# Patch extraction (im2col) on one core: two larger loads, stores of two channels throughout, and copies of three planes in one instruction

## Chip, cores, metric

One core of a Trainium2 chip. The metric is the device time of one execution in microseconds (us). The profile's span, from the first to the last instruction, is shorter than the device time of the same run (90.1 against 91.84). Most runs of one kernel agree within a few tenths of a per cent; a run over 1.5% above the fastest of its kernel counts as slow and is left out of the ratios.

## The reference, cut to what matters

```python
x = randn(16, 64, 32, 32) float32;  kernel_size = 3
for b in range(16):
    for i in range(30):
        for j in range(30):
            cols[b, :, i * 30 + j] = x[b, :, i:i+3, j:j+3].ravel()      # cols: (16, 576, 900) float32
```

Nothing is computed. Each input channel (32 × 32) appears nine times in the output, as nine planes of 30 × 30: plane (ki, kj) is the window that starts at row ki and column kj. 4.19 MB are read and 33.18 MB are written.

## The kernel before

Each of the 128 partitions holds eight channels (32 KB). For each channel nine copies build the planes in an output tile, and the tile goes out in long contiguous runs. There are two output buffers of two channels each, and all transfers are issued from one queue (SP).

```python
in_tile = in_pool.tile([P, CPP, H, W], x.dtype, name="in_tile")          # CPP = 8 channels
out_pool = ctx.enter_context(tc.tile_pool(name="out_pool", bufs=2))
cuts = [0, H, 200, CPP * H]                     # 4 KB, 21 KB and 7 KB per partition
first = load(nc.sync, cuts[0], cuts[1])
bulk = load(nc.sync, cuts[1], cuts[2])
load(nc.sync, cuts[2], cuts[3])

on_act = (False, True, False, True, False)
n = 0
for c in range(0, CPP, 2):
    out_tile = out_pool.tile([P, 2, KK, HO, WO], x.dtype, name="out_tile")
    for s in range(2):
        for kk in range(KK):
            ki, kj = divmod(kk, K)
            src = in_tile[:, c + s, ki : ki + HO, kj : kj + WO]
            dst = out_tile[:, s, kk]
            if on_act[n % len(on_act)]:
                nc.scalar.copy(out=dst, in_=src)
            else:
                nc.vector.tensor_copy(out=dst, in_=src)
            n += 1
        if c == 0:
            st = nc.sync.dma_start(out=out_v[:, s], in_=out_tile[:, s]...)      # one channel
            if s == 0:
                tc.add_manual_dep(st.ins, bulk.ins.name, ...,
                                  reason="the store follows the bulk of the loads")
    if c > 0:
        nc.sync.dma_start(out=out_v[:, c : c + 2]..., in_=out_tile...)          # two channels
# ... afterwards the first load is moved to the head of the program
```

## Time and profile before

| | kernel before |
|---|---|
| device time, median of the 6 runs taken with the changed kernel | 91.72 us (91.44 to 92.87, the highest counted as slow; medians of later rounds 91.54 to 91.56) |
| span of the profiled run (device time 91.84 us) | 90.1 us |
| VectorE / ScalarE busy | 23.5 / 26.2 us |
| DMA engines busy | 97.0% |
| first load packet / first store packet / last packet's end | 1.01 / 11.54 / 88.78 us |

How to read it: the two copy engines idle most of the time, the DMA engines hardly ever. The times of the last line come from the packet records of the trace (each packet's size, start and duration). The profiled run is 0.3 us above the later medians. Its records show one reason: 33 of the 128 packets of the bulk load (21,504 bytes) took 0.83 to 1.38 us instead of 0.80, which adds up to 0.24 us on each DMA engine, at a time when no store had been issued. No run here shows why. The prediction shows the profile's own lines.

### The profile page before, as it was taken

The page shows a single profiled execution, that of the slowest core. Times are in us where ns is not written, and L with a number is a line of the kernel's source. Part 1 is how long each engine was busy: PE and PEld are TensorE (multiplying, and loading weights), DVE is VectorE, ACT ScalarE, POOL GpSimd, SP SyncE. Part 2 cuts the span into 40 slices and gives each one's busy share as a digit, 9 for nine tenths or more (in the row PEclk, how much of TensorE's full clock was granted, in tenths as well). Part 3 has the DMA queues.
Part 4 walks back from the last instruction along what each step waited for, and adds up shares of the span by engine and source line. Part 5 has one row for each costly group of instructions (what it writes and reads, how often), then busy time and mean ns, then how long its engine had stood idle before and what let it go on. Part 6 is the DMA issues. An engine that isn't in the chain of part 4 may idle for free.

```text
span 90.1 us, 140 instructions
## 1 busy us (share of the span) xinstructions
DVE 23.5 (26%) x43; ACT 26.2 (29%) x30; POOL 0.2 (0%) x4
## 2 busy tenths in 40 slices
DVE  0380399970000089600000399300000000000000
ACT  5391399940000089920000399300000000000000
POOL 0000000000000000000000000000000000000000
DMA  5999899999599999993799999999999999947990
GB/s 129 486 382 449 360 518 446 460 460 446 259 460 460 691 460 432 460 432 173 345 460 460 460 460 460 460 460 460 460 460 460 460 432 460 403 201 345 460 460 0
DMA packets 1152, 37.37 MB, mean 415 GB/s; under 512 B 128, under 2 KB 128, under 8 KB 384
## 3 DMA queue, kind: packets, MB, share of 16 engines
q1 hardware_dynamic: 1152, 37.37, 97.0%
HBM read 4.19 MB, written 33.18 MB: 415 GB/s over the span
## 4 chain that ended last, share of the span: by engine, by line
DMA 45%; DVE 16%; DVEq 1%; issue 0%; SPq 0%
DMA out_dram<-out_tile 35%; DVE out_tile L57 16%; DMA in_tile<-in_x_dram 11%; DVEq L93 1%; DVEq L57 0%; SPq L75 0%
## 5 line engine op out<-in xcount | busy, mean ns | idle before, releaser
L55 ACT COPY out_tile<-in_tile 128x900 f32<-128x900 f32 x29 | 24.9, 938 | 30.1 <-DMA out_dram<-out_tile 25.3
L57 DVE COPY out_tile<-in_tile 128x900 f32<-128x900 f32 x43 | 23.5, 624 | 33.6 <-DMA out_dram<-out_tile 26.0
L55 ACT ACT_TABLE_LOAD x1 | 1.3, 1283 | 0.8 <-PEq L122 0.8
L122 POOL MEMSET const-bfloat16-1.0<- 128x1 bf16 x1 | 0.1, 102 | 0.0
L122 POOL MEMSET const-uint8-127<- 128x1 uint8 x1 | 0.1, 102 | 0.0
L122 POOL MEMSET const-float32-0.0<- 128x1 f32 x1 | 0.1, 99 | 0.2 <-issue 0.2
L122 POOL MEMSET const-float32-1.0<- 128x1 f32 x1 | 0.1, 99 | 0.0
## 6 DMA issues: line engine op xcount, KB each, us to landing
out_dram<-out_tile SPq DMA_DIRECT2D x3, 8100.0 KB, 31.3
out_dram<-out_tile SPq DMA_DIRECT2D x2, 4050.0 KB, 14.9
in_tile<-in_x_dram SPq DMA_DIRECT2D x1, 2688.0 KB, 9.6
in_tile<-in_x_dram SPq DMA_DIRECT2D x1, 896.0 KB, 11.4
in_tile<-in_x_dram SPq DMA_DIRECT2D x1, 512.0 KB, 3.6
```

The source lines that it names most:

```text
L55: nc.scalar.copy(out=dst, in_=src)
L57: nc.vector.tensor_copy(out=dst, in_=src)
L93: tc.compile()
L122: nc = _bacc.Bacc("TRN2", target_bir_lowering=False, num_devices=1)
```

## The change

The intent: fewer and larger operations. Two loads instead of three (8 and 24 KB per partition, cut into packets of at most 12 KB), four equal stores of two channels each, and 28 copies of up to three planes instead of 72 of one. The three windows of one row offset ki start at columns 0, 1 and 2, so a source view with a leading step of one element covers all three; the three planes of the destination are neighbours.

```diff
-    cuts = [0, H, 200, CPP * H]
-    first = load(nc.sync, cuts[0], cuts[1])
-    bulk = load(nc.sync, cuts[1], cuts[2])
-    load(nc.sync, cuts[2], cuts[3])
+    first = load(0, 2 * H)                  # both with max_dma_last_dim=12288
+    load(2 * H, CPP * H)
+
+    def windows(c, ki, kj, n):
+        w = in_tile[:, c, ki : ki + HO, kj : kj + WO]
+        part, row, col = [list(d) for d in w.ap]
+        return bass.AP(w.tensor, w.offset, [part, [1, n], row, col])
 
-    on_act = (False, True, False, True, False)
-    n = 0
+    units = (                               # channel of the pair, ki, kj, planes, on ScalarE?
+        (0, 0, 0, 3, False),
+        (0, 1, 0, 3, True),
+        (0, 2, 0, 3, False),
+        (1, 0, 0, 3, True),
+        (1, 1, 0, 3, False),
+        (1, 2, 2, 1, True),
+        (1, 2, 0, 2, False),
+    )
     for c in range(0, CPP, 2):
         out_tile = out_pool.tile([P, 2, KK, HO, WO], x.dtype, name="out_tile")
-        ... nine single-plane copies per channel; at c == 0 one store per channel,
-            the first of them with a wait on the bulk load; at c > 0 one store per pair
+        for s, ki, kj, n, on_act in units:
+            src = windows(c + s, ki, kj, n)
+            dst = out_tile[:, s, ki * K + kj : ki * K + kj + n]
+            if on_act:
+                nc.scalar.copy(out=dst, in_=src)
+            else:
+                nc.vector.tensor_copy(out=dst, in_=src)
+        nc.sync.dma_start(out=out_v[:, c : c + 2]..., in_=out_tile...)
```

More of the change, by code (lines that the diff above doesn't have):

```diff
@@ L19, in _im2col @@
     CPP = B * C // P
-    assert CPP * P == B * C and C % CPP == 0 and CPP % 4 == 0
+    assert CPP * P == B * C and C % CPP == 0 and CPP % 2 == 0 and K == 3
     x_v = x.rearrange("b (cp c2) h w -> (b cp) (c2 h w)", c2=CPP)
@@ L31, in _im2col, with load @@
     in_flat = in_tile.rearrange("p c h w -> p (c h w)")
-    def load(queue, r0, r1):
-        return queue.dma_start(
-            out=in_flat[:, r0 * W : r1 * W], in_=x_v[:, r0 * W : r1 * W]
-        )
-    cuts = [0, H, 200, CPP * H]
-    first = load(nc.sync, cuts[0], cuts[1])
-    bulk = load(nc.sync, cuts[1], cuts[2])
-    load(nc.sync, cuts[2], cuts[3])
-    on_act = (False, True, False, True, False)
-    n = 0
+    def load(r0, r1):
+        return nc.sync.dma_start(
+            out=in_flat[:, r0 * W : r1 * W],
+            in_=x_v[:, r0 * W : r1 * W],
+            max_dma_last_dim=12288,
+        )
@@ L48, in _im2col @@
         out_tile = out_pool.tile([P, 2, KK, HO, WO], x.dtype, name="out_tile")
-        for s in range(2):
-            for kk in range(KK):
-                ki, kj = divmod(kk, K)
-                src = in_tile[:, c + s, ki : ki + HO, kj : kj + WO]
-                dst = out_tile[:, s, kk]
-                if on_act[n % len(on_act)]:
-                    nc.scalar.copy(out=dst, in_=src)
-                else:
-                    nc.vector.tensor_copy(out=dst, in_=src)
-                n += 1
-            if c == 0:
-                st = nc.sync.dma_start(
-                    out=out_v[:, s],
-                    in_=out_tile[:, s].rearrange("p kk i j -> p (kk i j)"),
-                )
-                if s == 0:
-                    tc.add_manual_dep(
-                        st.ins,
-                        bulk.ins.name,
-                        mybir.DependencyInfo(
-                            mybir.DependencyClass.Sync, mybir.DependencyReason.DATA
-                        ),
-                        reason="the store follows the bulk of the loads",
-                    )
@@ L74, in _im2col @@
-        if c > 0:
-            nc.sync.dma_start(
-                out=out_v[:, c : c + 2].rearrange("p c n -> p (c n)"),
-                in_=out_tile.rearrange("p c kk i j -> p (c kk i j)"),
-            )
+        for s, ki, kj, n, on_act in units:
[5 more added lines that the diff above has]
+                nc.vector.tensor_copy(out=dst, in_=src)
@@ L79, in _im2col @@
+        nc.sync.dma_start(
+            out=out_v[:, c : c + 2].rearrange("p c n -> p (c n)"),
+            in_=out_tile.rearrange("p c kk i j -> p (c kk i j)"),
+        )
     return first
```

## The prediction

The recorded text is cut where that is marked: what it said of the hardware without a trace of this case is gone, and with it terms of the forecast's sum. What they came to: 2.97 us for a copy of three planes on VectorE and 1.09 for one of two, which make the 9.7 us per pair, and 2.44 us for three planes on ScalarE, which make the 5.6. The whole sum then runs 4.8 + 9.7 = 14.5, store packets from 15.6, a span of 93.9 and **95.3 us**. "The fallback" and "a slow VectorE" stand for the copies of 2.97 us. Rival A put the same copy at 1.56 us, and at 2.03 if the destination kept its three planes apart.

> **What bounds the kernel now.** I read the queue totals first, then the chain that ended last, then the groups by line, then the timeline.
>
> ```profile
> span 90.1 us, 140 instructions
> DVE 23.5 (26%) x43; ACT 26.2 (29%) x30; POOL 0.2 (0%) x4
> q1 hardware_dynamic: 1152, 37.37, 97.0%
> ```
>
> The two copy engines work for about a quarter of the span each; the 16 DMA engines are busy for 97.0% of it. They move 37.37 MB, which is 37.37 MB / 16 = 2.336 MB per DMA engine. The packet records of the trace give the rate: a store packet of 64,800 bytes takes 2.394 us, one of 32,400 takes 1.200 us, a load packet of 21,504 takes 0.799 us and one of 4,096 takes 0.159 us. That is 25.8 to 27.1 bytes per ns, so size hardly matters from 4 KB up. At 27.1 the traffic alone is 2.336 MB / 27.1 = 86.3 us. First packet: 1.0 us after the span's start. Last packet: 88.8 us. After it there are 1.3 us of tail. So 90.1 = 1.0 + 87.8 + 1.3, and only 87.8 - 86.3 = 1.5 us are lost between first and last packet (a slow first packet per engine, packet overheads, one engine that ends 0.35 us behind the rest). **The kernel runs at the pace of its DMA queue, and what can be won is at most some 1.5 us.** What can be lost is any time in which the queue runs dry.
>
> The chain of waits, in order of time, shows where the queue could run dry:
>
> ```profile
> 0.79 9.62 DMA in_tile<-in_x_dram
> 10.43 9.24 DVE out_tile L57 x17
> ...
> 19.74 31.24 DMA out_dram<-out_tile
> ...
> 52.26 4.84 DVE out_tile L57 x9
> ```
>
> This chain goes through VectorE between 10.43 and 19.74, but those copies do not hold up the DMA engines: the two single-channel stores run at that time. The timeline says so:
>
> ```profile
> 3.61 3.48 ACT L55 COPY out_tile<-in_tile 128x900 f32<-128x900 f32 x4 [1.54 <-DMA in_tile<-in_x_dram]
> 3.61 2.78 DVE L57 COPY out_tile<-in_tile 128x900 f32<-128x900 f32 x5 [3.61 <-DMA in_tile<-in_x_dram]
> 10.43 8.54 ACT L55 COPY out_tile<-in_tile 128x900 f32<-128x900 f32 x10 [3.35 <-DMA in_tile<-in_x_dram]
> 10.43 9.23 DVE L57 COPY out_tile<-in_tile 128x900 f32<-128x900 f32 x17 [4.04 <-DMA in_tile<-in_x_dram]
> 10.50 3.67 SPq L60 DMA_DIRECT2D out_dram<-out_tile  x2
> 19.74 37.77 SPq L75 DMA_DIRECT2D out_dram<-out_tile  x3
> ```
>
> Channel 0 is copied from 3.61 us, while the loads are still running. Its store waits only for the bulk load and is issued at 10.50. The last load packets end at 11.6 to 12.2, and the first store packets start at 11.5: there is no gap. That is the **critical hand-over**: the first store must be ready by about 10.6 us. All later stores are issued some 12 us before the store ahead of them ends (19.74 against 31, about 39 against 51, 57.5 against 70), so there is much slack there.
>
> The last view is the cost of a copy:
>
> ```profile
> L55 ACT COPY out_tile<-in_tile 128x900 f32<-128x900 f32 x29 | 24.9, 938 | 30.1 <-DMA out_dram<-out_tile 25.3
> L57 DVE COPY out_tile<-in_tile 128x900 f32<-128x900 f32 x43 | 23.5, 624 | 33.6 <-DMA out_dram<-out_tile 26.0
> ```
>
> VectorE takes 624 ns for 900 fp32 elements. ScalarE takes 938. In back-to-back runs the pitch is (9.23 - 0.62) / 16 = 538 ns on VectorE and (8.54 - 0.94) / 9 = 844 ns on ScalarE, so neighbours overlap by some 86 and 93 ns.
>
> [...]
>
> **The change, part by part.**
>
> *Loads.* The bytes are the same. The packets become 128 of 8 KB and 256 of 12 KB instead of 4, 21 and 7 KB. By the packet times above this is worth some 0.1 us. The first load is twice as long: 8 packets of 8,192 bytes on each engine instead of 8 of 4,096, so 32,768 / 27.1 = 1.2 us more. The first copies then start at 3.6 + 1.2 = **4.8 us** and the loads still end near 11.7.
>
> *Stores.* Two stores of one channel become one of two channels. One issue less costs nothing on a full queue. But now the first store needs all 18 planes of the first pair, where only 9 were needed before.
>
> *Copies.* Per pair, VectorE has three copies of three planes and one of two (11 planes). ScalarE has two of three and one of one (7 planes). [...] 2 × 2.44 + 0.94 - 2 × 0.09 = **5.6 us** per pair.
>
> VectorE is the disputed cost. The three planes of the destination lie side by side, and since 30 rows of 30 were folded into a run of 900, I expect a run of 2,700 (even). The three source windows start one element apart, so they cannot be folded: the source is 3 × 30 × 30 with an outermost 3. [...] The pair: 3 × 2.97 + 1.09 - 3 × 0.09 = **9.7 us**.
>
> *The hand-over.* The first pair is ready at 4.8 + 9.7 = 14.5 us. The store is issued at 14.6, and its first packets run about 1.0 us later (the first load took 1.0 us from issue to first packet): 15.6 us. The loads ended near 11.7, so the DMA engines stand idle for some 3.9 us that were filled before. From there on it is the old stream: before, the stores ran from 11.5 to 88.8, 77.2 us with the stagger that the loads left. After: 15.6 + 77.0 + 1.3 = **93.9 us** of span, 3.8 more.
>
> *Later pairs.* Pair 2 is copied from 14.5 to 24.3 while store 1 runs to about 35. Pair 3 starts when store 1 frees its buffer and is ready at about 45, with store 2 running to 54. Pair 4 is ready about 64 of 73. A slow VectorE has 9 us to spare in each, so the fallback costs only once, at the start.
>
> The device time was 91.5 with a span near 90.1, so I add the same 1.4 to 1.5: 93.9 + 1.4 = **95.3 us**, 4% slower.
>
> **Rivals.** (A) [...] a pair 3 × 1.56 + 1.09 - 0.26 = 5.5 us, about ScalarE's 5.6. The store would be issued near 10.5 as today, with no gap, and the time would be 91.2 to 91.6. For it speaks that the split of 11 to 7 planes is balanced only at this rate, so the author counted on it[...]. If the destination stayed 3 × 900 (odd and equal), [...] 2.03 us each, a pair in 6.9 us, store issued at 11.8, about 1 us of gap, 92.4 us. Together 22%. (B) *The gap is filled anyway.* Nothing else is in the queue then: the loads are all issued in the first 2 us and no other store is ready. I give it nothing beyond A. (C) *The hand-built source view makes the first copies wait for both loads.* Channels 0 and 1 lie wholly in the first load, and today the copies of channel 0 wait for their own load only, so I doubt it. It would start copies near 12.2 and cost another 7 us: 102 us. 5%. (D) *Larger load packets or fewer stores win something.* All that is lost inside the stream is 1.5 us of 90.1, less than 2%, so a gain over 2% is all but excluded.
>
> **Range and chances.** The main path spans 94.5 to 96.3 (some 0.4 us of doubt about the issue latency and 0.5 about the copies). Rival A pulls the low end down to 91.3. I take 91.3 to 96.4. Slower by over 2% (above 93.3): main path plus C, 0.76. Within 2%: 0.22. Faster: 0.02.
>
> **What would show it.** Right: VectorE's three-plane group at about 2,970 ns and its two-plane group at about 1,090; VectorE busy near 40 us instead of 23.5; first copies at about 4.8; the first store issued at 14 to 15; a DMA dip in the slices around 12 to 15.6 us and full slices afterwards; the last store landing 3.4 to 4 us later than before. Wrong: a three-plane mean near 1,560 or 2,030 ns with the first store issued by 12 us (rival A), or first copies near 12 us (rival C). Load packets that move slower than 26 bytes per ns, or store packets above 2.40 us, would mean that the stream itself changed, which I do not expect.

## The result and the profile after

The changed kernel takes **95.16 us** (95.08 to 95.21, six runs), the kernel before 91.72 us in the same rounds. The ratio is 1.037 (95% interval 1.033 to 1.041): slower. Here and below a ratio is the mean time of one kernel's fast runs over that of the other's fast runs of the same rounds, so it is not quite the ratio of the medians quoted.

From the page of the changed kernel: the totals, two of the rows in 40 slices (busy share in tenths; a slice is 2.33 us), and the queue.

```profile
span 93.3 us, 88 instructions
DVE 38.8 (42%) x16; ACT 23.8 (26%) x13; POOL 0.2 (0%) x4
...
DVE  0099999999300009999200069994000000000000
...
DMA  5999809999999999999966899999999999999990
...
q1 hardware_dynamic: 992, 37.37, 93.3%
```

The bytes are the same 37.37 MB, but the queue is busy for 93.3% of a longer span instead of 97.0%. The sixth digit of the DMA row is a 0: between 11.7 and 14.0 us the DMA engines do nothing (0 GB/s), and VectorE is at 9 in that slice. The page counts a packet's whole time in the slice in which the packet starts (so a stretch can show a share above 1: 1.21 from 14 to 16 us). So the 9 after the 0 hides that the gap goes on to 15.36 us, where the first store packets start. The two digits 6 in the middle of the stream are not a second gap: the 32 store packets of an engine take 76.6 us by their records, and the stores last 76.8 from the first packet to the last. A store packet (2.395 us) is a little longer than a slice, so each of the 16 engines has one slice in which no packet starts: four slices there have 15, 10, 10 and 13 starts instead of 16.

The groups by line with the shapes kept apart (count, then busy us and mean ns) give the durations that the prediction turned on:

```profile
L68 DVE COPY out_tile<-in_tile 128x2700 f32<-128x2700 f32 x12 | 34.8, 2958 | 25.3 <-DMA out_dram<-out_tile 20.6 <-DMA in_tile<-in_x_dram 4.7
L66 ACT COPY out_tile<-in_tile 128x2700 f32<-128x2700 f32 x8 | 19.2, 2442 | 35.4 <-DMA out_dram<-out_tile 31.0 <-DMA in_tile<-in_x_dram 4.4
L68 DVE COPY out_tile<-in_tile 128x1800 f32<-128x1800 f32 x4 | 4.4, 1088 | 0.0
```

On VectorE the two-plane copy costs 0.60 ns per element and the three-plane copy 1.10. ScalarE shows no such step: 0.90 ns per element for three planes, and 1.04 for one (938 ns). A line through these two means (938 ns for 900 elements, 2,442 for 2,700) has 0.84 ns per element and 186 ns fixed; that is an estimate from two points.

The timeline (start, duration, then what; the duration of a row with several issues reaches from the first to the last):

```profile
4.70 5.63 ACT L66 COPY out_tile<-in_tile 128x2700 f32<-128x2700 f32 x3 [2.63 <-DMA in_tile<-in_x_dram]
4.70 19.34 DVE L68 COPY out_tile<-in_tile 128x2700 f32<-128x2700 f32 x8 [4.70 <-DMA in_tile<-in_x_dram]
12.07 5.64 ACT L66 COPY out_tile<-in_tile 128x2700 f32<-128x2700 f32 x3 [1.74 <-DMA in_tile<-in_x_dram]
14.51 49.99 SPq L69 DMA_DIRECT2D out_dram<-out_tile  x4
```

ScalarE has its share of the first pair at 10.33 us; VectorE goes on to 14.4. The first store is issued at 14.51 and its first packet starts at 15.36, while the last load packet ended at 11.64. The gap is 15.36 - 11.64 = 3.7 us, and the last packet ends at 92.15 instead of 88.78.

The chain that ended last must be read with care here:

```profile
4.70 19.35 DVE out_tile L68 x8
...
24.11 30.14 DMA out_dram<-out_tile
```

It lays 19.35 us on VectorE, two pairs of copies. Only the first pair's 9.7 us set the end. The second pair is copied while store 1 occupies the DMA engines. The experiments show that directly.

### The profile page after: what moved, and what is told of

The parts are those of the page before. It is cut to its first block, busy times and chain, and to the rows that moved or that the text cites. A ratio compares the mean times of both kernels' runs of the same rounds, so it can differ in the third digit from the quotient of the medians.

```text
span 93.3 us, 88 instructions
## 1 busy us (share of the span) xinstructions
DVE 38.8 (42%) x16; ACT 23.8 (26%) x13; POOL 0.2 (0%) x4
## 2 busy tenths in 40 slices
DMA packets 992, 37.37 MB, mean 401 GB/s; under 512 B 96, under 2 KB 96, under 8 KB 96
## 3 DMA queue, kind: packets, MB, share of 16 engines
q1 hardware_dynamic: 992, 37.37, 93.3%
## 4 chain that ended last, share of the span: by engine, by line
DMA 37%; DVE 28%; DVEq 3%; issue 0%; SPq 0%
DMA out_dram<-out_tile 32%; DVE out_tile L68 28%; DMA in_tile<-in_x_dram 5%; DVEq L87 3%; DVEq L68 0%; SPq L69 0%
## 5 line engine op out<-in xcount | busy, mean ns | idle before, releaser
L68 DVE COPY out_tile<-in_tile 128x2700 f32<-128x2700 f32 (+1 forms) x16 | 38.8, 2491 | 25.3 <-DMA out_dram<-out_tile 20.6
L66 ACT COPY out_tile<-in_tile 128x2700 f32<-128x2700 f32 (+1 forms) x12 | 22.5, 1940 | 35.4 <-DMA out_dram<-out_tile 31.0
```

## The experiments

The trace lists how each copy's operands were encoded, as counts per dimension: the three-plane copy has 3 × 30 × 30 as its source and one run of 2,700 as its destination. The outermost count is the first of these. Dimensions that together form one contiguous run were merged into it (here called folded).

The theory: VectorE's three-plane copy takes 2,958 ns because of how it is encoded, with outermost counts of 3 (source) and 2,700 (destination, folded into one run). That makes the first pair ready only at 14.4 us, the DMA engines idle between the loads and the first store, and the gap passes one for one into the end. The rivals: overlapping windows in one instruction are slow whatever their order; VectorE's greater work counts in every pair; the loads or the wider first store cost something by themselves.

### Same three planes, rows outermost

```diff
-        return bass.AP(w.tensor, w.offset, [part, [1, n], row, col])
+        return bass.AP(w.tensor, w.offset, [part, row, [1, n], col])
...
+            dst = dst.rearrange("p n i j -> p i n j")
```

> Same three-plane copies as the changed kernel, but the 30 rows are walked outermost (30 on both sides, even) and the three planes inside. Theory (the outermost count decides the VectorE rate, and the late first store is all of the loss): [...] first pair ready near 10.3 us, first store packets at about 11.5 us with no gap behind the loads, 91.4 to 91.9 us, as the kernel before. Rival (three overlapping windows in one instruction are slow in themselves): copies stay near 2.9 us and the time near 95.1.

(Expected about 1.56 us for a three-plane copy on VectorE instead of 2.96.)

Measured: 91.39 us (91.30 to 91.46, six runs), ratio to the kernel before 0.9975 (0.9956 to 0.9994). The group of VectorE's three-plane copies (ScalarE's are reordered too and hardly move, 2,463 ns after 2,442):

```profile
L73 DVE COPY out_tile<-in_tile 128x2700 f32<-128x2700 f32 x12 | 18.1, 1561 | 34.1 <-DMA out_dram<-out_tile 27.4 <-DMA in_tile<-in_x_dram 6.7
```

Its timeline around the first store:

```profile
4.87 5.52 DVE L73 COPY out_tile<-in_tile 128x2700 f32<-128x2700 f32 x4 [4.87 <-DMA in_tile<-in_x_dram]
10.56 46.11 SPq L74 DMA_DIRECT2D out_dram<-out_tile  x4
```

Both sides are now encoded as 30 × 3 × 30. The same windows, the same overlap, as many elements and instructions, and 1,561 ns instead of 2,958. So neither the three windows nor their overlap are slow; what made the difference in this pair of runs is how the copy is encoded, with rows or with planes outermost. The first store packet starts at 11.43 us and the whole loss is gone.

### Mended in the first pair only, and in the later pairs only

```diff
+            rows_outer = c == 0        # first run;  c > 0 in the mirror image
```

> The rows-outermost copies in the first channel pair only; the later three pairs keep the slow copies of the changed kernel. Theory (a slow VectorE costs only at the first hand-over): within 0.3 us of the kernel with all pairs mended, 91.4 to 91.9 us. Rival (VectorE's 39 us of work slows the stream everywhere, by its own time or by contention with the stores): some three quarters of the loss stays, about 94.2 us.

Measured: 91.38 us (91.27 to 91.47), ratio 0.9974.

> The mirror image: slow copies in the first pair, rows-outermost copies in the later three. Theory: VectorE's busy time falls by some 12 us (9 copies by 1.4) and the time does not move: 95.0 to 95.3 us. Rival (the work of VectorE counts everywhere): about 92.5 us.

Measured: 95.18 us (95.05 to 95.37), ratio 1.0392. The totals of the two:

```profile
span 89.5 us, 88 instructions
DVE 34.7 (39%) x16; ACT 23.9 (27%) x13; POOL 0.2 (0%) x4
```

```profile
span 93.4 us, 88 instructions
DVE 26.2 (28%) x16; ACT 23.9 (26%) x13; POOL 0.2 (0%) x4
```

The kernel with 34.7 us of VectorE work is the fast one and the kernel with 26.2 us the slow one. Three slow copies at the start cost 3.8 us; nine later ones cost nothing that these runs can see. That disposes of the rival "VectorE's work counts everywhere", and of any cost of the slow copies through contention with the stores.

### Slow copies kept, the first store split

```diff
+        if c == 0:
+            for s in range(2):
+                nc.sync.dma_start(out=out_v[:, s], in_=out_tile[:, s]...)
+        else:
             nc.sync.dma_start(out=out_v[:, c : c + 2]..., in_=out_tile...)
```

> The changed kernel with its slow copies everywhere; only the first store is split again into one store for each of the two channels. Theory (the loss is the product of slow copies and of a first store that waits for 18 planes): channel 0 is complete after two slow copies, at 4.7 + 2.96 + 2.88 = 10.5 us, its store's packets start near 11.6, the gap is gone, 91.5 to 92.0 us although no copy is faster. Rival (the slow copies cost by themselves, or the larger loads do): 94 to 95.2 us.

Measured: 91.52 us (91.42 to 91.63), ratio 0.999 (0.9969 to 1.0012). VectorE still takes 2,958 ns for each three-plane copy and is busy for 38.8 us:

```profile
L68 DVE COPY out_tile<-in_tile 128x2700 f32<-128x2700 f32 x12 | 34.8, 2958 | 21.7 <-DMA out_dram<-out_tile 16.9 <-DMA in_tile<-in_x_dram 4.8
```

But channel 0 is complete after two of them:

```profile
10.74 4.20 SPq L71 DMA_DIRECT2D out_dram<-out_tile  x2
```

Its packets start at 11.59, and the loads end at 11.75. So the loss needs both parts of the change: copies that are slow, and a first store that waits for all of them. Either one alone is free here.

### One of three slow copies mended

```diff
+            rows_outer = c == 0 and (s, ki) == (1, 1)
```

> Dose: of the first pair's three slow copies only one is mended (rows outermost), everything else as in the changed kernel. Theory (each microsecond of the first pair on VectorE beyond the hand-over is a microsecond of the end): 1.4 us less than the changed kernel, 93.6 to 93.9 us, and the first store packet near 14.0 us instead of 15.4. Rival (the loss is a step, a wait that either is there or is not): 91.4 or 95.1.

Measured: 93.87 us (93.83 to 93.95), ratio 1.0249; first store packet at 14.15 us. The loss is not a step: 1.4 us less on VectorE before the first store are 1.3 us less in the median (in the two profiled runs the first packet moves by 1.2, and the first copies happened to start 0.18 us later in this one).

### An odd outermost count on both sides

Planes one below the other (same kj, ki = 0, 1, 2) lie three planes apart in the output, so they cannot be folded, and both sides have an outermost 3.

```diff
-        return bass.AP(w.tensor, w.offset, [part, [1, n], row, col])
+        return bass.AP(w.tensor, w.offset, [part, [W, n], row, col])
...
+            dst = out_tile[:, s].rearrange("p (a b) i j -> p b a i j", b=K)[:, kj, ki : ki + n]
# ... and the list of units names the same planes by columns instead of by rows
```

> Three planes one below the other instead of side by side (same column offset, three row offsets): the destination planes then lie 2,700 elements apart and can't be folded, so source and destination both have an outermost count of 3, odd and equal. [...] copies stay at 2.96 us and the time at 95.1. [...] the first pair at 4.8 + 6.9 = 11.7 us, first store packets near 12.5 against loads that end near 11.5, 92.2 to 92.6 us. [...] 1.56 us and 91.4 us.

(Three outcomes were named: 2.96 us per copy and 95.1 us; 2.03 us per copy and 92.2 to 92.6 us; 1.56 us per copy and 91.4 us.)

Measured: 92.38 us (92.32 to 92.48), ratio 1.0087, first store issued at 11.80, its first packet at 12.65.

```profile
L68 DVE COPY out_tile<-in_tile 128x2700 f32<-128x2700 f32 x12 | 23.6, 2023 | 31.0 <-DMA out_dram<-out_tile 25.7 <-DMA in_tile<-in_x_dram 5.3
```

2,023 ns is neither 2,958 nor 1,561; it is the second of the expected outcomes. So an outermost 3 alone does not make the copy as slow as in the changed kernel: 3 against a folded 2,700 takes 2,958 ns, 3 against 3 takes 2,023. The runs show these durations and not what in VectorE is behind them.

### The loads alone

The kernel before with the two loads of the change, and without the first store's extra wait on the bulk load.

```diff
-    cuts = [0, H, 200, CPP * H]           # and the three loads
+    first = load(0, 2 * H)
+    load(2 * H, CPP * H)
...
-                if s == 0:
-                    tc.add_manual_dep(st.ins, bulk.ins.name, ...)
```

> The kernel before with only the two loads of the change (8 KB and 24 KB per partition, packets of 8 and 12 KB); its single-plane copies and its two single-channel first stores stay; the first store's extra wait on the bulk load goes[...]. Theory (the stream's rate is what it was, and channel 0 is ready near 8.5 us, before the loads end): 91.3 to 91.6 us. Rival (the larger first load costs its 1.2 us of later start): 92.7 us.

Measured: 92.29 us (92.17 to 92.60, six runs), ratio 1.0081 (1.0062 to 1.0101). **Missed**, by both theories: the first copies did start 1.3 us later, but channel 0 was ready long before the loads ended.

```profile
4.89 6.01 DVE L57 COPY out_tile<-in_tile 128x900 f32<-128x900 f32 x11 [4.89 <-DMA in_tile<-in_x_dram]
...
8.39 2.93 SPq L60 DMA_DIRECT2D out_dram<-out_tile  x2
```

The store is issued at 8.39 us, while loads are running. The packet records show 12 KB load packets of 0.46 us as everywhere else up to 9.9 us, and then some 40 between 0.48 and 1.01 us, mostly near 0.75; the loads end at 12.51 us instead of 11.64 to 11.83. I had taken the wait out on the belief that the order of the queue makes it needless, which no run had shown. The new question: is it the loads, or the store issued among them?

### The wait of the kernel before, taken out by itself

```diff
                 st = nc.sync.dma_start(out=out_v[:, s], ...)
-                if s == 0:
-                    tc.add_manual_dep(st.ins, bulk.ins.name, ...)
```

> The kernel before, loads and all, with only the first store's extra wait on the bulk load taken out (its data wait stays). The store is then issued near 7.2 us into a queue that still holds some 4 us of loads. Theory formed after the loads-only run, which was 0.7 us slower and whose load packets stretched from 0.46 to some 0.75 us about 1.5 us after the early store's issue: a store queued behind running loads slows them, so some load packets take well over their 0.80 us and the time is about 92.2 us. Rival (the 8 and 24 KB loads themselves did it): 91.4 to 91.7.

Measured: 92.77 us (92.74 to 93.13), ratio 1.0141 (1.0116 to 1.0166), so the wait is worth 1.2 us to the kernel before. Right in kind, larger than expected, and in other packets than I had said: most of the bulk load's packets still take 0.80 us. Six after 8.3 us take about 1.0, but such packets stretch in the profile of the kernel before as well, and more of them (33 against 12 over 0.83 us), so they are weak evidence about the store. The 7 KB packets are better: 79 of 128 take over 0.30 us, none in the kernel before. They belong to the last load and stretch from a median of 0.272 us to 0.415, up to 0.87. The store's issues:

```profile
7.07 6.62 SPq L60 DMA_DIRECT2D out_dram<-out_tile  x2
```

The first store packet starts at 12.79 instead of 11.54. Two views of stretches of time (8 to 10 and 10 to 12 us; after the length come the busy times of VectorE, ScalarE and GpSimd, the clock, the share of DMA time and GB/s, where a packet's time and bytes are counted at its start), first of the kernel before, then of this one:

```profile
8.00:10.00 2.00, 0.00 (x0) 0.00 (x0) 0.00 (x0) 1.00 0.73 308
10.00:12.00 2.00, 1.57 (x3) 1.57 (x2) 0.00 (x0) 1.00 1.36 576
```

```profile
8.00:10.00 2.00, 0.05 (x1) 0.05 (x1) 0.00 (x0) 1.00 0.86 272
10.00:12.00 2.00, 2.00 (x4) 2.00 (x3) 0.00 (x0) 1.00 0.90 197
```

With the store queued at 7.07, the DMA engines look as busy (0.90) between 10 and 12 us and take up only 197 GB/s. Store packets that begin late in this stretch swell the 576 of the kernel before, so the packet durations above are the better measure.

### The loads alone, with the wait

```diff
-    load(2 * H, CPP * H)
+    bulk = load(2 * H, CPP * H)          # and the manual wait of the first store on it, as before
```

> The loads-only kernel with the first store's wait put on the second load. Load packets should stay at 0.46 us. But this wait ends only when all loads have landed, near 11.9 us, so the first store packets start near 12.9: a gap of about 1.1 us, and 92.4 to 92.7 us. If the time is 91.5 the issue latency was hidden in another way.

Measured: 92.98 us (92.97 to 93.05), ratio 1.0153; the load packets are all at 0.46 us again and end at 11.74, as expected. The time is 0.3 us above the expected range (a miss in size): the landing is seen only at 12.2 and the first store packet starts at 13.10, 1.36 us behind the loads:

```profile
12.24 0.83 SPq L60 DMA_DIRECT2D out_dram<-out_tile  x2
```

So the loads are innocent: what stretched them was the early store. And waiting for the very last load overshoots. The kernel before is cut so that its wait ends with the bulk load, with 0.9 MB still to come to hide the store's start (issued at 10.50, first packet at 11.54; the last load packet ends at 12.21).

### The change without its three-plane copies

```diff
 # the two loads and four two-channel stores of the change,
 # with the single-plane copies of the kernel before
```

> The change without its three-plane copies: its two loads, its four two-channel stores, and the single-plane copies of the kernel before. Theory: the pair is ready at 4.8 + 6.0 = 10.9 us, first store packets at 11.8 behind loads that end at 11.7, so 91.4 to 91.7 us; fewer and longer copies are worth nothing here, and the three-plane form is all of the loss. Rival (the loads or the wider first store carry part of the loss): above 92 us.

Measured: 91.53 us (91.42 to 91.55, six runs), ratio 0.999 (0.9974 to 1.0006). The pair is ready at 10.9 us, the first store packet starts at 11.79, the loads end at 11.78.

```profile
4.85 6.00 DVE L57 COPY out_tile<-in_tile 128x900 f32<-128x900 f32 x11 [4.85 <-DMA in_tile<-in_x_dram]
10.94 46.29 SPq L59 DMA_DIRECT2D out_dram<-out_tile  x4
```

With all else as in the changed kernel, the three-plane copies on VectorE are the whole loss. Fewer instructions bring nothing: 132 instructions here, 88 with rows outermost, and 0.15% between their ratios (0.999 and 0.9975, intervals that overlap).

### Load packets of 24 KB

```diff
-            max_dma_last_dim=12288,       # in the rows-outermost kernel
```

> The rows-outermost kernel without the 12 KB cap, so that the second load moves in packets of 24 KB. Theory (size hardly matters from 4 KB up): the same 91.4 us within 0.2. Rival (the cap is what made the rows-outermost kernel 0.2 us faster than the kernel before): 91.6 us or above, with slower or staggered load packets.

Measured: 91.26 us (91.17 to 91.31, six runs), ratio 0.9963 (0.9948 to 0.9978). The 24 KB packets take 0.912 us, twice the 0.460 of 12 KB. The two rows-outermost kernels ran in different rounds and their intervals overlap, so no effect of the cap is shown. This is the fastest version, 0.4% under the kernel before: no gain of note, as the bound allows.

### All of it in one table

First and last packet times are from the packet records of each profiled run, in us. The last three rows stand outside the order: the kernel before, and the two kernels whose first store was issued early.

| kernel | first store issued | its first packet | last packet's end | device time (median) |
|---|---|---|---|---|
| rows outermost, 24 KB packets | 10.46 | 11.31 | 88.18 | 91.26 |
| rows outermost, first pair only | 10.42 | 11.29 | 88.20 | 91.38 |
| rows outermost | 10.56 | 11.43 | 88.34 | 91.39 |
| first store split | 10.74 | 11.59 | 88.48 | 91.52 |
| single planes | 10.94 | 11.79 | 88.61 | 91.53 |
| odd and equal | 11.80 | 12.65 | 89.46 | 92.38 |
| loads alone, with wait | 12.24 | 13.10 | 89.97 | 92.98 |
| one copy mended | 13.29 | 14.15 | 90.93 | 93.87 |
| changed kernel | 14.51 | 15.36 | 92.15 | 95.16 |
| rows outermost, later pairs only | 14.64 | 15.50 | 92.28 | 95.18 |
| kernel before (its profiled run: 91.84) | 10.50 | 11.54 | 88.78 | 91.54 to 91.72 |
| loads alone | 8.39 | 11.92 | 89.05 | 92.29 |
| kernel before without its wait | 7.07 | 12.79 | 89.65 | 92.77 |

The last packet ends 76.8 to 76.9 us after the first store packet in every row but two. In the loads alone (77.1) and the kernel before (77.2) the last load packets still ran for 0.6 and 0.7 us after the first store packet had started on another engine. Eight packets of 64,800 bytes in each of four stores (or the same bytes in shorter ones) make 32 × 2.395 = 76.6 us on each engine, so nothing is left between them: once started, the stream never runs dry. The moment at which it starts is all that sets these kernels apart, but for those 0.2 to 0.4 us.

## Why the prediction was right, step by step

The time (95.3 against 95.16), the direction and the mechanism held. By its steps:

- **The bound.** Held. Store packets are 2.395 us after and 2.394 before. No version gained more than 0.4%. Two slips changed nothing: 2.336 MB at 27.1 bytes per ns are 86.2 us, not 86.3, and the list of what is lost in the stream leaves out the stretched bulk packets (0.24 us). The third of the issues compared with the store ahead is at 57.17 us; the 57.5 of the text is where that row of the timeline ends.
- **Three-plane copies of 2.97 us.** Held: 2,958 ns against about 2,970 forecast, with the two-plane copy (2 against a run of 1,800) at 1,088 (about 1,090). The rows-outermost (1,561 ns) and the odd-and-equal (2,023 ns) runs show that the encoding, and not the size or the overlap, is behind it; the trace's operands are encoded as forecast, 3 × 30 × 30 against one run of 2,700. The reason that the forecast gave for its durations was not shown. Rival A did not come true for this kernel, but its sums did where an experiment made its conditions true: 1.56 us per copy and 91.2 to 91.6 us (rows outermost: 1.561 and 91.39), 2.03 us, issue at 11.8 and 92.4 us (odd and equal: 2.023, 11.80 and 92.38).
- **First copies at 4.8 us.** 4.70. This also refutes rival C: the hand-built view waits for the first load only.
- **First store issued at 14.6, first packet at 15.6.** 14.51 and 15.36. The latency from issue to first packet was put at 1.0 us from the first load; for a store on an empty queue it is 0.85 to 0.86 (the five runs of the table whose first store is issued at 11.80 us or later).
- **77.0 us of stream and 1.3 of tail.** 76.8 and 1.15. These small excesses add up: a span of 93.9 was forecast, and it is 93.3. The step from span to device time was mis-sized the other way, 1.4 forecast and 1.8 measured. I had set the span of a run of 91.84 us against 91.5. The two errors largely cancel, so it is partly luck that the final number agrees better than its terms.
- **The later pairs are free.** Held, and shown in both directions. Pair 4 was ready at 64.1 us, as forecast.
- **"Nothing else is in the queue" (rival B).** Held for this change: the slice of zero.
- **What it did not see.** It took the first store's wait on the bulk load as a mere delay ("its store waits only for the bulk load") and did not ask what the wait is for. It protects the loads: without it the kernel before is 1.2 us slower. In the changed kernel that loss does not appear, because its store comes after the loads anyway (issued at 14.51, loads ended at 11.64). In the mended versions the store is issued near 10.5 us, some 1.2 us before the loads end, and no load packet stretches (with rows outermost the DMA engines take 430 GB/s at a share of 1.01 from 10 to 11 us, which makes 0.46 us for 12 KB).

Open: why a store queued behind running loads stretches their packets. That it does so was shown in two kernels with different loads; the cause no run here shows. Also open is how early is too early: issues at 10.4 to 10.9 us did no harm, those at 7.1 and 8.4 did. The packet records narrow it. After those two early issues the first clear stretching appears in load packets that start 1.6 us after the issue (loads alone) and 2.3 us after it (kernel before without its wait), or 1.3 if the six doubtful bulk packets count. In the mended versions the last load packet starts at most 0.8 us after the issue. So they may have escaped only because their loads were nearly over.

## What to carry to other kernels

In a kernel that runs at the pace of its DMA queue, look first for the moment at which loads end and stores begin: what had to be finished by then counted microsecond for microsecond here (rows outermost against the changed kernel: first store packet 3.9 us later, end 3.8 later), and the same work later took nearly twice as long unseen (nine copies of 2,958 ns instead of 1,561: 91.38 us against 91.39). Before several fp32 copies on VectorE are joined into one, write down the counts of source and destination as they will be encoded, after neighbouring dimensions have been folded (planes that lie side by side in the destination fold on that side alone), and time the same copy with another dimension outermost: for the same 2,700 elements 3 against a folded run took 2,958 ns, 3 against 3 2,023, and 30 against 30 1,561. And before a wait that looks redundant is removed, measure it alone: here it was worth 1.2 us.
